# A decoder trunk on one core: three pool column tiles by groups of 256 tokens, early weights, a norm row by DMA, and three kept pairs of f tiles

## The chip, the core and the metric

The kernel runs on one core of a Trainium2 chip. The metric is the device time of one launch in microseconds; a time of the kernel is the median of several runs. The engines in the profile are PE (the matmul engine), DVE (vector), ACT (scalar), POOL (GpSimd) and SP, which here only issues DMAs.

## What is computed

One layer of a decoder on 1024 tokens of width 1024, in fp32. The input projection feeds three mixers; this is the reference cut to what the change touches:

```python
u = rmsnorm(x, norm_mix)
(pool_v, q, k, v, f_logit, z, xbc, dt_raw, gate_logits) = split_columns(u @ w_in)
y_pool = pool_mixer(pool_v, pool_mix, pool_scale) @ p_pool   # four groups of 128 columns
y_attn = forgetting_attention(q, k, v, f_logit, f_bias) @ p_attn
y_ssd  = ssd_mixer(z, xbc, dt_raw, ...) @ p_ssd
x = x + (g[0] * y_pool + g[1] * y_attn + g[2] * y_ssd) @ w_out
x = x + conv_ffn(rmsnorm(x, norm_ffn), ffn_up, ffn_conv_w, ffn_conv_b, ffn_down)
out = rmsnorm(x, norm_final)
```

The pool mixer takes, for each of its four groups, a trailing mean over 2, 4, 8 or 16 tokens, subtracts the token itself, multiplies by a 128 x 128 matrix and scales.

## The kernel before, in words

Every fp32 product is made of three matmuls on PE (`mm3`, L117): the high half of a weight with the high half of the data, the high half with the low, the low half with the high. A weight tile of 128 x 1024 comes by `load_w` (L107): SP issues its DMA into `wraw`, ACT casts it to `whi` (L112), DVE subtracts to `wlo` (L105). There is one `wraw` buffer, and there are three pairs of `whi` and `wlo`.

PSUM has two kinds of tiles here, set by `psum`: `big`, 1024 columns of fp32, which is two banks, and `bank`, 512 columns. Two of `big` and four of `bank` are set at first. A tile is taken when a buffer of its kind is free, and comes free with its last reader.

**The start (L207 to L228).** SP requests the eight tiles of x, 128 tokens each. The norm of a tile is a sum of squares on ACT (L150), a reciprocal root with a Newton step (`rstd`, L127 to L143, one column, mostly on DVE) and a product on DVE with the norm row (`n_xn`, L152). The norm row lies in `nm`, a `big` tile that four matmuls (L218) fill from a row of one partition. `to_T` turns the tile on PE, eight transposes into two `bank` tiles (L160); ACT casts the high half `uh` (L162) and DVE makes the low half `ul` (L105).

**Column tiles.** `in_proj` computes 128 columns of the projection for all tokens into one `big` tile, in groups of 512 tokens or of 256 (the first two pool tiles). After the second tile stand the f and dt projection (L303 to L393: softplus on DVE, then sums over tokens on PE, L362 to L366, copied by DVE into `acs`, `cum` and `tot`, and a running offset `off` that goes into `cum`).

**The pool mixers (L397 to L438).** For each of four groups: ACT copies the column tile out of PSUM to `va` (two buffers, L409), POOL makes the first shifted sum `vs` and DVE the others (L416), DVE makes the difference in `va` (L420). For each half of the tokens ACT casts `dh`, DVE makes `dl`, PE multiplies by the group's matrix into a `bank` tile (three matmuls: `dh` with `mixh`, `dl` with `mixh`, `dh` with `mixl`), ACT makes `yph` (L433) and DVE `ypl` (L435) from it. Then come the convolution tiles of the SSD mixer (`p_big`, in_proj again).

**The end (L1123 to L1237).** The FFN's down projection goes over eleven groups of f tiles, each a pair. For the last 512 tokens the last `NL` pairs are kept and `last_down` goes over them in two parts of 256 tokens, `qs[0]` and `qs[1]`, block by block (j = 4 to 7), each block with an add to x (L1224) and a square that goes into the sum of squares (L171, L172). `last_norm` makes the final norm of such a part: sums over partitions on PE (L179), the reciprocal root on DVE, its spread on PE (L185), eight products (L1187) and the output DMAs. `step` puts pieces of the norm of `qs[0]` among the blocks of `qs[1]`.

The order of the instructions on each engine is chosen by the framework's scheduler when the program is built; it is fixed in the program, and each engine goes through its own list.

## Time and profile before

| | us |
|---|---|
| median of three runs (lowest, highest) | 1877.31 (1876.27, 1879.17) |
| the profiled execution | 1876.14 |
| its span | 1874.4 |
| PE busy | 1841.7 (98%) |
| DVE busy | 1086.6 (58%) |
| ACT busy | 856.8 (46%) |

A row of the timeline gives the start in the span, the duration, and in brackets how long the engine stood idle before it and which instruction ended that. PE's matmuls overlap, so the distance between two starts, not the duration, is what one more costs. PEclk is the clock that PE was granted, 1.00 being full speed.

### The profile page before, as it was taken

The numbers are of one execution on the slowest core, as the hardware profiler recorded it, in microseconds if no ns is written. First come the engines' busy times: TensorE is split into PE (matmuls) and PEld (weight loads), VectorE is DVE, ScalarE is ACT, GpSimd is POOL, SyncE is SP. The second block draws the span as 40 slices with busy tenths as digits, with TensorE's granted clock in tenths as the row PEclk, the third lists the DMA queues.
The fourth block names the chain that finished last, engine by engine and source line by source line (L and its number), as shares of the span: only waits on it lengthen the run. The fifth ranks groups of instructions, "written<-read, shape, count | busy, mean of one in ns | idle before, by whom it ended". The sixth has DMA issues, their size and how long they took to land.

```text
span 1874.4 us, 22365 instructions
## 1 busy us (share of the span) xinstructions
PE 1841.7 (98%) x8622; PEld 1504.7 (80%) x8622; DVE 1086.6 (58%) x1611; ACT 856.8 (46%) x1384; POOL 157.1 (8%) x119
## 2 busy tenths in 40 slices
PE   7999999999999999999999999999999999999997
PEld 6888888888878778787788888878888888888886
DVE  6752682661265553655765432878787887743424
ACT  5343584573255463654633322545454555533221
POOL 0100240330000000000022002320000000000000
PEclk9999999999999999999999999999999999999998
DMA  4231231333511313124364451443333321664532
GB/s 153 84 120 34 85 108 57 101 130 104 175 65 62 107 51 129 40 90 153 121 200 135 145 180 68 152 135 124 102 107 118 104 91 53 214 235 157 180 102 68
DMA packets 81629, 217.35 MB, mean 116 GB/s; under 512 B 8625, under 2 KB 15217, under 8 KB 80754
## 3 DMA queue, kind: packets, MB, share of 16 engines
q1 hardware_dynamic: 76192, 201.82, 31.9%
q0 software_dynamic: 1728, 8.39, 1.4%
q10 hardware_dynamic: 3602, 5.72, 0.9%
q8 instruction: 67, 1.10, 0.2%
q14 instruction: 40, 0.33, 0.1%
HBM read 164.41 MB, written 51.48 MB: 115 GB/s over the span
## 4 chain that ended last, share of the span: by engine, by line
PE 93%; DVE 2%; DMA 2%; ACT 1%; issue 1%; POOL 0%; SPq 0%; DVEq 0%; ACTq 0%; POOLq 0%
PE p_bank L123 40%; PE p_big L123 19%; PE p_half L123 17%; PE p_bank L265 2%; PE p_bank L264 2%; PE p_bank L263 2%; PE p_po L722 2%; PE p_sc L674 2%; PE p_pt L697 2%; PE p_bank L557 1%; PE p_sc L673 1%; PE p_bank L1068 0%; DMA yi<-yn_d 0%; PE p_bank L324 0%; DMA ab<-in_f_up_dram 0%
## 5 line engine op out<-in xcount | busy, mean ns | idle before, releaser
L105 DVE TENSOR_TENSOR wlo<-wraw,whi 128x1024 fp32r<-128x1024 f32 (+1 forms) x109 | 126.3, 1159 | 162.8 <-ACT whi L112 161.3
L123 PE MATMUL p_bank<-act,whi 128*128 128x512 f32 (+1 forms) x736 | 218.5, 381 | 0.0
L123 PE MATMUL p_big<-uh,whi 128*128 128x512 f32 (+1 forms) x416 | 157.4, 379 | 0.5 <-ACT whi L112 0.5
L123 PE MATMUL p_big<-uh,wlo 128*128 128x512 f32 (+1 forms) x416 | 157.2, 378 | 0.5 <-DVE wlo L105 0.5
L123 PEld LDWEIGHTS p_bank<-act,whi 128*128 128x128 f32 x736 | 136.0, 188 | 26.6
L123 PE MATMUL p_big<-ul,whi 128*128 128x512 f32 (+1 forms) x416 | 156.7, 377 | 0.0
L123 PE MATMUL p_half<-uh,whi 128*128 128x512 f32 x384 | 153.4, 399 | 0.0
L123 PE MATMUL p_half<-ul,whi 128*128 128x512 f32 x384 | 153.0, 399 | 0.0
L123 PE MATMUL p_half<-uh,wlo 128*128 128x512 f32 x384 | 152.2, 397 | 0.0
L112 ACT CAST whi<-wraw 128x1024 fp32r<-128x1024 f32 x81 | 84.9, 1048 | 137.6 <-PE p_big L123 68.4
L123 PE MATMUL p_bank<-act,wlo 128*128 128x512 f32 (+1 forms) x368 | 139.2, 381 | 0.0
L123 PE MATMUL p_bank<-t,whi 128*128 128x512 f32 x440 | 137.2, 391 | 0.0
L123 PE MATMUL p_bank<-b,whi 128*128 128x512 f32 x376 | 118.9, 397 | 2.2 <-ACT whi L1046 2.0
L1024 DVE SCALAR_TENSOR_TENSOR vg<-cc,vec,vg 128x1023 f32<-128x1023 f32 (+1 forms) x88 | 110.3, 1278 | 8.4 <-ACT vg L1022 8.3
L105 DVE TENSOR_TENSOR wlo<-stage,whi 128x1024 fp32r<-128x1024 f32 x44 | 54.1, 1230 | 101.2 <-ACT whi L112 101.0
L112 ACT CAST whi<-stage 128x1024 fp32r<-128x1024 f32 x44 | 46.1, 1051 | 115.2 <-PE p_bank L123 106.7
L123 PEld LDWEIGHTS p_bank<-t,whi 128*128 128x128 f32 x440 | 82.6, 188 | 17.8
L123 PE MATMUL p_bank<-t,ring 128*128 128x512 f32 x396 | 96.4, 391 | 0.0
L172 POOL TENSOR_TENSOR ss<-ss,vg 128x512 f32<-128x512 f32 (+1 forms) x21 | 30.0, 1429 | 763.7 <-ACT vg L171 763.5
L123 PEld LDWEIGHTS p_big<-uh,wlo 128*128 128x128 f32 x416 | 78.9, 190 | 14.6 <-DVE wlo L105 0.8
L123 PEld LDWEIGHTS p_big<-uh,whi 128*128 128x128 f32 x416 | 79.0, 190 | 14.2 <-ACT whi L112 0.9
L123 PEld LDWEIGHTS p_big<-ul,whi 128*128 128x128 f32 x416 | 79.0, 190 | 13.5
(307 smaller groups left out, 4067.7 us busy)
## 6 DMA issues: line engine op xcount, KB each, us to landing
ab<-in_f_up_dram SPq DMA_DIRECT2D x53, 512.0 KB, 3.3
wraw<-in_w_in_dram SPq DMA_DIRECT2D x48, 512.0 KB, 3.4
stage<-in_f_down_dram SPq DMA_DIRECT2D x44, 512.0 KB, 3.5
g_d<-gt SPq DMA_DIRECT2D x48, 256.0 KB, 2.0
gt<-g_d SPq DMA_DIRECT2D x48, 256.0 KB, 3.4
act_d<-vg SPq DMA_DIRECT2D x22, 512.0 KB, 3.0
stage<-act_d SPq DMA_DIRECT2D x22, 512.0 KB, 4.5
mt<-acs_d SPq DMA_DIRECT2D x16, 512.0 KB, 4.4
```

The source lines that it names most:

```text
L105: eng.tensor_tensor(lo, src, hi.bitcast(F32), op=ALU.subtract)
L112: nc.scalar.copy(hi, raw)
L123: m = nc.tensor.matmul(o, lhsT=wt, rhs=ah[part], start=first and i == 0, stop=last and i == 2, **kw)
L172: eng.tensor_tensor(ss, ss, sq, op=ALU.add)
L263: nc.tensor.matmul(ps, lhsT=a, rhs=hi[:, c], start=k == 0, stop=False)
L264: nc.tensor.matmul(ps, lhsT=a, rhs=lo[:, c], start=False, stop=False)
L265: nc.tensor.matmul(ps, lhsT=ul[t // 4][:, k, q], rhs=hi[:, c], start=False, stop=k == NT - 1)
L557: nc.tensor.matmul(py[:, d], lhsT=mt[:, h * P:(h + 1) * P], rhs=xd[:, d], start=True, stop=True)
L674: nc.tensor.matmul(pss[:, 0:w], lhsT=Q2[h][hp, qs], rhs=KL[hp, j0:j0 + w], start=False, stop=True)
L697: nc.tensor.transpose(pt[:, off + (i - qq[0]) * P:off + (i - qq[0] + 1) * P], in_=probs[i][:, kb * P:(kb + 1) * P], identity=ident)
L722: nc.tensor.matmul(po[:, q0:q0 + w], lhsT=VV[:, kb, h, :], rhs=t[:, o:o + w], start=pc == 0 and i == 0, stop=last and i == len(prods) - 1)
L1024: nc.vector.scalar_tensor_tensor(out=acc[:, s:], in0=c[:, 0:1024 - s], scalar=w[2 - s], in1=acc[:, s:], op0=ALU.mult, op1=ALU.add)
```

## The change

Four things change. In the first stage PSUM is split into three `big` and two `bank` tiles; the old split comes back after the pool mixers. The norm row is spread to all partitions by a DMA into SBUF, and the four matmuls go. The weights of the first three pool tiles are requested behind the second, third and fourth tile of x, and these three tiles are computed together, group of 256 tokens by group; the third was computed by groups of 512 before. `in_proj` loses its width. At the end three pairs are kept instead of two, and the pieces of the norm of `qs[0]` stand after block 4, after block 5 and after blocks 6 and 7.

```diff
-    psum(big=(1024, 2), bank=(512, 4))
+    psum(big=(1024, 3), bank=(512, 2))
...
-    nm_row = spool.tile([1, 1024], F32, name="nm_row", bufs=1)
-    nc.scalar.dma_start(nm_row, row_in[:, R_NM:R_NM + 1024])
+    nm = spool.tile([P, 1024], F32, name="nm", bufs=1)
+    nc.scalar.dma_start(nm, row(R_NM, 1024))
...
-        nm = big()
-        for h in range(2):
-            nc.tensor.matmul(nm[:, h * 512:(h + 1) * 512], lhsT=ones[0:1, :], rhs=nm_row[:, h * 512:(h + 1) * 512],
-                             start=True, stop=True)
         xns = []
+        first_w = []
         for i in range(NT + 1):
             if i < NT:
                 xt = sp.tile([P, 1024], F32, name="xt", bufs=8)
                 nc.sync.dma_start(xt, x_t[i])
+                if i in (1, 2, 3):
+                    first_w.append(load_w(w_in[T_POOL + i - 1]))
                 xns.append(norm(sp, xt, nm, 4))
...
+        first = [big() for _ in first_w]
+        for t0 in range(0, S, 256):
+            h, q = t0 // 512, slice(t0 % 512, t0 % 512 + 256)
+            for ps, (hi, lo) in zip(first, first_w):
+                for k in range(NT):
+                    c = slice(k * P, (k + 1) * P)
+                    mm3([ps[:, t0:t0 + 256]], (hi[:, c], lo[:, c]), [(uh[h][:, k, q], ul[h][:, k, q])],
+                        k == 0, k == NT - 1)
         for g, w in enumerate(WINDOWS):
-            ps = in_proj(T_POOL + g, 256 if g < 2 else 512)
+            ps = first[g] if g < len(first) else in_proj(T_POOL + g)
...
+    psum(big=(1024, 2), bank=(512, 4))
...
-        NL = 2
+        NL = 3
...
-        m = step(m, last_down(qs[1], (5, 6)))
+        m = step(m, last_down(qs[1], (5,)))
         m = step(m, n)
-        m = step(m, last_down(qs[1], (7,)))
+        m = step(m, last_down(qs[1], (6, 7)))
```

SP's list now begins with two tiles of x, a weight, the other six tiles of x, the mixers' matrices and three weights; before, all eight tiles of x stood first. PE's list begins with 16 transposes ahead of the first column tile, where there were the four matmuls of L218 and 32 transposes.

Where the scheduler puts things further on is seen in three places. In the rows that follow, lines are those of each program; a number behind a name is that of its buffer's tile.

**PE in the pool mixers.** Here `p_big_909` and `p_big_954` are the fourth column tile, `p_big_1014` and `p_big_1067` the first convolution tile, and `p_bank_845`, `859`, `883` (before `783`, `797`) results of the mixers' products. Before:

```order
L123 MATMUL p_big_909<-uh1_85,wlo_906 128x512
L123 MATMUL p_big_1014<-uh0_84,whi_1010 128x512
L388 MATMUL p_bank_509<-cst_75,cumh_507 64x128
L123 MATMUL p_bank_783<-dh_779,mixh_524 128x512
L123 MATMUL p_big_1014<-ul0_86,whi_1010 128x512
L123 MATMUL p_big_1014<-uh0_84,wlo_1011 128x512
L123 MATMUL p_big_1014<-uh0_84,whi_1010 128x512
L123 MATMUL p_big_1014<-ul0_86,whi_1010 128x512
L123 MATMUL p_bank_783<-dl_781,mixh_524 128x512
L123 MATMUL p_bank_783<-dh_779,mixl_526 128x512
L123 MATMUL p_bank_797<-dh_793,mixh_524 128x512
L123 MATMUL p_big_1014<-uh0_84,wlo_1011 128x512
```

After:

```order
L123 MATMUL p_big_954<-uh1_85,wlo_951 128x512
L385 MATMUL p_bank_524<-cst_75,acs_360 128x128
L123 MATMUL p_bank_845<-dh_841,mixh_539 128x512
L123 MATMUL p_bank_845<-dl_843,mixh_539 128x512
L123 MATMUL p_bank_845<-dh_841,mixl_541 128x512
L123 MATMUL p_bank_859<-dh_855,mixh_539 128x512
L123 MATMUL p_bank_859<-dl_857,mixh_539 128x512
L123 MATMUL p_bank_859<-dh_855,mixl_541 128x512
L123 MATMUL p_bank_883<-dh_879,mixh_539 128x512
L123 MATMUL p_bank_883<-dl_881,mixh_539 128x512
L123 MATMUL p_bank_883<-dh_879,mixl_541 128x512
L123 MATMUL p_big_1067<-uh0_84,whi_1063 128x512
```

Before, the products of the second group stand among the matmuls of the convolution tile. After, the products of three halves follow each other, between the fourth column tile and the convolution tile.

**DVE in the pool mixers**, from the copy of the sums on (`acs`, `cum`, `tot`). Before:

```order
L370 COPY acs_345<-p_bank_483 128x128
L371 COPY cum_349<-p_bank_483 128x64
L368 COPY tot_487<-p_bank_485 128x192
L375 TENSOR_TENSOR off_491<-off_491,tot_487 128x8
L380 TENSOR_TENSOR dd_503<-tot_487,acs_345 128x128
L375 TENSOR_TENSOR off_491<-off_491,tot_487 128x8 x3
L382 TENSOR_TENSOR dtd_347<-dtt_344,dd_503 128x128
L375 TENSOR_TENSOR off_491<-off_491,tot_487 128x8
L416 TENSOR_TENSOR vs_868<-vs_865 128x1024
L375 TENSOR_TENSOR off_491<-off_491,tot_487 128x8
L416 TENSOR_TENSOR vs_871<-vs_868 128x1024
```

After:

```order
L368 COPY acs_360<-p_bank_498 128x128
L369 COPY cum_364<-p_bank_498 128x64
L366 COPY tot_502<-p_bank_500 128x192
L423 TENSOR_TENSOR vs_916<-vs_913 128x1024
L421 MEMSET vs_1006 128x16
L373 TENSOR_TENSOR off_506<-off_506,tot_502 128x8
L378 TENSOR_TENSOR dd_518<-tot_502,acs_360 128x128
L105 TENSOR_TENSOR wlo_1188<-wraw_1185,whi_1187 128x1024
L425 TENSOR_TENSOR vs_916<-vs_916,cst_75 128x16
L421 MEMSET vs_1009 128x16
L373 TENSOR_TENSOR off_506<-off_506,tot_502 128x8
L442 SCALAR_TENSOR_TENSOR ypl_851<-p_bank_845,vec_82,yph_849 128x512
```

After the copies now come a weight's low half and a second shifted sum before the first `ypl`; six rows further, `va_907`, and then `ypl_865` and `dl_895`, follow.

**DVE at the end**, where the norm of `qs[0]` and the last blocks meet. Before:

```order
L1224 TENSOR_TENSOR x2h_13376<-x2h_13376,p_bank 128x256
L140 TENSOR_TENSOR rs_t<-rs_t,rs_v 128x2
L141 TENSOR_SCALAR rs_t<-rs_t 128x2
L143 TENSOR_TENSOR rs_r<-rs_y,rs_t 128x2
L172 TENSOR_TENSOR ss<-ss,vg 128x256
L1224 TENSOR_TENSOR x2h_13376<-x2h_13376,p_bank 128x256
L1187 SCALAR_TENSOR_TENSOR x2h_13376<-x2h_13376,vec,p_st 128x256 x8
L172 TENSOR_TENSOR ss<-ss,vg 128x256
L1224 TENSOR_TENSOR x2h_13376<-x2h_13376,p_bank 128x256
L172 TENSOR_TENSOR ss<-ss,vg 128x256
```

After:

```order
L141 TENSOR_SCALAR rs_t<-rs_t 128x2
L1232 TENSOR_TENSOR x2h_13429<-x2h_13429,p_bank 128x256
L143 TENSOR_TENSOR rs_r<-rs_y,rs_t 128x2
L172 TENSOR_TENSOR ss<-ss,vg 128x256
L1195 SCALAR_TENSOR_TENSOR x2h_13429<-x2h_13429,vec,p_st 128x256 x8
L1232 TENSOR_TENSOR x2h_13429<-x2h_13429,p_bank 128x256 x2
L172 TENSOR_TENSOR ss<-ss,vg 128x256 x2
L181 TENSOR_REDUCE rs_n<-p_st 128x2
```

L1187 has become L1195 and L1224 has become L1232. The add of a block now stands right ahead of L143, the last step of the reciprocal root, and two adds stand behind the eight products, with their sums of squares after them.

## Rows read from the trace of the kernel before

**Rows 1.** The page: busy time of each engine; the last chain, by engine.

```profile
PE 1841.7 (98%) x8622; PEld 1504.7 (80%) x8622; DVE 1086.6 (58%) x1611; ACT 856.8 (46%) x1384; POOL 157.1 (8%) x119
...
PE 93%; DVE 2%; DMA 2%; ACT 1%; issue 1%; POOL 0%; SPq 0%; DVEq 0%; ACTq 0%; POOLq 0%
```

**Rows 2.** Waits of PE in 0 to 130 us: total, times, longest, us.

```profile
PE p_big L218 <- DMA cst<-in_cst_dram: 6.8, 1, 6.8
PE p_bank L160 <- DVE n_xn L152: 2.8, 2, 1.4
PE p_bank L160 <- DVE rs_y L134: 2.3, 1, 2.3
```

**Rows 3.** Windows: length; busy of PE, PEld, DVE, ACT, POOL; PEclk; DMA; GB/s.

```profile
20.00:25.00 5.00, 4.06 (x18) 3.36 (x17) 4.85 (x12) 3.38 (x8) 0.00 (x0) 0.50 0.27 88
...
35.00:40.00 5.00, 3.73 (x32) 3.77 (x33) 4.33 (x9) 2.42 (x4) 0.00 (x0) 1.00 0.40 128
```

**Rows 4.** PE instructions by group, 0 to 36.2 us; xcount, busy, mean ns.

```profile
L160 PE MATMUL p_bank<-cst,n_xn 128*128 128x128 f32 x56 | 9.7, 330 | 3.7 <-DVE rs_y L134 2.3 <-DVE n_xn L152 1.4
L123 PE MATMUL p_big<-uh,whi 128*128 128x256 f32 x24 | 7.6, 319 | 0.5 <-ACT whi L112 0.5
```

**Rows 5.** Timeline: start, us, instruction, [idle before]; PE's last early wait.

```profile
36.27 1.06 PE L160 MATMUL p_bank<-cst,n_xn 128*128 128x128 f32 x8 [1.44 <-DVE n_xn L152]
```

**Rows 6.** Timeline of PE: neighbouring matmuls of 256 and of 512 columns.

```profile
27.54 0.28 PE L123 MATMUL p_big<-uh,whi 128*128 128x256 f32 x1
27.66 0.28 PE L123 MATMUL p_big<-ul,whi 128*128 128x256 f32 x1
...
63.00 0.39 PE L123 MATMUL p_big<-ul,whi 128*128 128x512 f32 x1
...
63.23 0.39 PE L123 MATMUL p_big<-uh,wlo 128*128 128x512 f32 x1
```

**Rows 7.** Timeline of DVE in the start.

```profile
25.50 1.28 DVE L152 SCALAR_TENSOR_TENSOR n_xn<-xt,rs_r,p_big 128x1024 f32<-128x1024 f32 x1
...
26.99 1.23 DVE L105 TENSOR_TENSOR wlo<-wraw,whi 128x1024 fp32r<-128x1024 f32 x1
...
29.39 0.69 DVE L105 TENSOR_TENSOR ul<-p_bank,uh 128x512 fp32r<-128x512 f32 x1
```

**Rows 8.** The page, DMA issues: KB each, us to landing.

```profile
mt<-acs_d SPq DMA_DIRECT2D x16, 512.0 KB, 4.4
```

**Rows 9.** Timeline in the pool mixers: DVE, then PE, then ACT.

```profile
56.33 1.51 DVE L345 TENSOR_SCALAR den<-e 128x192 f32<-128x192 f32 x1 [0.33 <-ACT e L343]
...
74.86 0.29 DVE L370 COPY acs<-p_bank 128x128 f32<-128x128 f32 x1 [0.29 <-PE p_bank L364]
...
78.48 1.23 DVE L416 TENSOR_TENSOR vs<-vs 128x1024 f32<-128x1024 f32 x1
...
79.98 1.22 DVE L420 SCALAR_TENSOR_TENSOR va<-vs,va 128x1024 f32<-128x1024 f32 x1
...
81.25 0.74 DVE L435 SCALAR_TENSOR_TENSOR ypl<-p_bank,vec,yph 128x512 fp32r<-128x512 f32 x1
...
85.41 0.39 PE L123 MATMUL p_big<-uh,whi 128*128 128x512 f32 x1
...
86.33 1.01 ACT L409 COPY va<-p_big 128x1024 f32<-128x1024 f32 x1
```

**Rows 10.** Busy us by engine around a PE wait in the FFN; PEclk.

```profile
886.00:887.00 1.00, 0.23 (x1) 0.00 (x0) 0.37 (x2) 0.98 (x3) 0.00 (x0) 1.00 1.00 303
...
889.00:890.00 1.00, 1.00 (x5) 0.70 (x5) 0.00 (x0) 0.00 (x0) 0.00 (x0) 0.50 1.09 410
```

**Rows 11.** Timeline of the last tokens: DVE and PE.

```profile
1859.78 3.22 DVE L1187 SCALAR_TENSOR_TENSOR x2h<-x2h,vec,p_st 128x256 f32<-128x256 f32 x8
...
1860.78 0.28 PE L123 MATMUL p_bank<-act,wlo 128*128 128x256 f32 x1
...
1863.25 0.41 DVE L1224 TENSOR_TENSOR x2h<-x2h,p_bank 128x256 f32<-128x256 f32 x1
```

More of the change, by code (lines that the diff above doesn't have):

```diff
@@ L228, in hybrid_kernel, with in_proj @@
                 to_T(xns[t], uh[t // 4], ul[t // 4], (t % 4) * P)
-    def in_proj(t, width=512, after=None):
+    def in_proj(t, after=None):
         hi, lo = load_w(w_in[t], after=after)
         ps = big()
-        for t0 in range(0, S, width):
-            h, q = t0 // 512, slice(t0 % 512, t0 % 512 + width)
+        for h in range(2):
             for k in range(NT):
                 c = slice(k * P, (k + 1) * P)
-                mm3([ps[:, t0:t0 + width]], (hi[:, c], lo[:, c]), [(uh[h][:, k, q], ul[h][:, k, q])],
+                mm3([ps[:, h * 512:(h + 1) * 512]], (hi[:, c], lo[:, c]), [(uh[h][:, k, :], ul[h][:, k, :])],
                     k == 0, k == NT - 1)
```

## The prediction

> **What bounds the kernel now.** I read the page's busy shares and its chain of waits first [rows 1]: the matmul engine, PE, is busy for 1841.7 of 1874.4 us, and 93% of the chain that ends last lies on it. So an edit counts where it fills a hole of PE, opens one, or gives PE more to do. The list of PE's waits in the first 130 us gives the holes there [rows 2]: 6.8 us until the constants land, 2.8 and 2.3 us for the norm of x, and two of 0.5 us that are left out of the rows. All of them lie before 37 us; in the pool mixers PE runs without a hole today. The window table gives the state of PE's clock at the start [rows 3]: 0.50 of full speed, the lower of its two levels (1.2 of 2.4 GHz), in 20 to 25 us, right behind the 2.3 us hole, and full again later, as in 35 to 40 us.
>
> **The start: more work early, a little more work in all.** Before, PE leaves its last hole at 36.27 us [rows 5], with 24 matmuls of each of three kinds, 72 of 256 columns, and 56 transposes done [rows 4]. In the changed program the first matmul of a column tile stands behind 16 transposes instead of 32, and its weight is the third transfer on SP's queue. That start should come at some 14 to 15 us, but there is only one raw weight buffer, and the low half of the second weight is row 46 of DVE's queue. Ahead of it DVE has six norm products at 1.28 us, two low halves of weights at 1.23, six of x at 0.69 [rows 7], one of the mixers' matrix at about the same, and some 27 one-column operations at about 0.15: 7.7 + 2.5 + 4.1 + 0.7 + 4.0 = 19.0 us. The first product can start at about 6.8 us, so this half is there at 25 to 26 us; by the program's order PE then has only 27 matmuls and 32 transposes behind it. From there both tiles' groups keep PE fed. The missing 45 matmuls cost 45 x 0.12 = 5.4 us (27.54 to 27.66 in [rows 6]) and the missing 24 transposes 24 x 0.12 = 2.9 (eight in 1.06 less the tail of the last one, [rows 5]). PE is level with the old 36.27 at about 33.6 to 34: a gain of 2.3 to 2.7 us. Against it stands the narrower third tile: 48 matmuls of 512 columns become 96 of 256, and by [rows 6] a pair takes 0.24 against 0.23, so 48 x 0.01 = 0.5 us. The clock is the open term: short holes remain between 20 and 25 us, and at half speed until 28 instead of 25 PE would lose up to 1.6. The gain lies between 0.2 and 2.2 us; I take 1.2.
>
> The norm row now comes to all partitions by one DMA of 512 KB on ACT's queue, in place of four matmuls. The nearest row is a 512 KB read that is spread over the partitions in the same way, 4.4 us from issue to landing [rows 8]. Issued at 0.7 us it would land at 5 if alone; beside the x tiles, at up to 8, and the constants behind it follow. DVE then begins up to 1.2 us later and the whole start with it. So this term reaches from -2.2 to +1.0 us.
>
> **The pool mixers: a new hole.** This is the largest term. Three column tiles now hold three wide PSUM buffers, and only two banks are left for transposes, the f and dt work, and the mixers' products, where there were four. One of the two is held by the small tile with the summed decays (L385, then L388) until its last copy on DVE. The mixers' four first products therefore follow each other in the other bank. PE's queue has L385, then nine product matmuls in a row, and then the first convolution tile; before, its six products stood among the matmuls of the fourth tile.
>
> When does PE get there? Before, the convolution tile's first matmul starts at 85.41 [rows 9], with six product matmuls (1.4 us) and L387 ahead of it. Without these, and with 2.5 us gained at the start, PE ends the fourth tile at about 81.2 us. When does DVE? Before, it copies the sums at 74.86 and is free at once. After, the softplus chain starts later, because the f and dt matmuls stand behind three column tiles instead of two, by about 6.4 us; a mixer product va (1.22) and a shifted sum vs (1.23) of the next tiles stand ahead of the copy as well; a wait of DVE that was there before (2 us) is filled. So the copies come at about 82.3 us. Rows in which DVE takes 1.51 us for 192 columns while GpSimd adds [rows 9] lie in that stretch too, and three such additions crowd in.
>
> From the copies to the low half dl that frees the buffer va, DVE must do in this order: acs 0.29, cum 0.21, tot 0.35, vs 1.23, four short ones 0.6, dd 0.28, a weight's low half 1.23, ypl 0.74, dl 0.67, dtd 0.28, va 1.22, ypl 0.74, dl 0.67, in sum 8.5 us, and some 0.4 less since they overlap a little (those over a microsecond and ypl are in [rows 9], the weight's half in [rows 7], the short ones are read from the same view). It ends at about 90.4. Then ACT copies the fourth tile into va, 1.01 us [rows 9], and only that frees the wide buffer in which the convolution tile is to start: 91.4 us. Between 81.2 and 91.4 PE has L385 (0.1) and nine product matmuls (9 x 0.23 = 2.1, [rows 6]) to do. The hole is 10.2 - 2.2 = 8.0 us. It comes in four parts: about 1.6 us for the copy of cum, 3.0 for the first ypl, 2.1 for the second, 1.2 for the copy into va. Queued behind PE's waiting instruction is the whole convolution, which needs none of these results; nothing later gives the time back, as PE had no holes there that could shrink. If DVE comes to the copies earlier or later by 1 us, the hole is 7 to 9.
>
> The clock may add to this. After an idle stretch of 1.4 us at 886 us, in the middle of dense work, the granted clock was 0.50 until 892, some three microseconds, though PE was busy throughout [rows 10]; it was 0.50 after the 2.3 us hole at the start too [rows 3]; after the 1.44 us hole before 36.27 it stayed full [rows 3, 5]. Half speed for 3.4 us of dense work costs 1.7, and if two of the products run slow as well, 1.2 more, since DVE waits for them. Bounds 0 to 2.9; I take 1.7, the row at 886.
>
> The Trainium skill ("TensorE: Matmul & The Clock Gate", "A second HAM failure mode: psum-queue depth-cycling") says that cycling through PSUM banks makes PE idle briefly between groups of matmuls, often enough that the clock swings between its levels and throughput falls. The change halves the banks in this stretch, so the rule speaks against it. By it the sum would take the upper end of the clock's term instead of the middle.
>
> **The tail.** Three pairs of f tiles instead of two are kept for the last 512 tokens. That turns 24 matmuls of 512 columns into 48 of 256: 24 x 0.01 = 0.25 us more. The two steps of the second half that follow the first half's norm now hold 36 matmuls instead of 12, so that the eight products of the norm (3.22 us, from 1859.78) lie beside PE work. Before, the last matmul starts at 1860.78 and ends at 1861.06, but its add stands behind these eight and a sum of squares and starts at 1863.25 [rows 11]. After, the add follows at once: -2.1 us. Against that, the last step of the reciprocal root (L143) now stands behind the add of block 5, and PE's L185 waits for it: an add 0.41 (as in [rows 11]), a small product 0.16, and two hand-overs make 0.7 us. Net -2.1 + 0.25 + 0.7 = -1.15; between -0.5, if the last weight's halves come late, and -1.6, if PE's last short matmuls keep the full clock. I take -1.2. The third kept weight needs the buffer of the last group before it; other matmuls cover its cast and its low half, 1.0 and 1.2 us, with 28 or more ahead of them in PE's queue (3.3 us); without that cover it would cost up to 2.3.
>
> **The sum.** Start -1.2, hole +8.0, clock +1.7, tail -1.2: +7.3 us. The profiled execution took 1876.14 us, so 1883.4 by it; it is 1.2 below the median of the runs, 1877.31, so 1884.6 on that. I say 1884.5. All good ends together (-2.2, +7.0, 0, -1.6) give 1880.5, all bad ones (+1.0, +9.0, +2.9, -0.5) 1889.7.
>
> **Rivals.**
> *The hole is covered (faster side).* If DVE reached the copy of cum by some 73 to 74 us, as it does now, the ypl and dl would be done before PE ends the fourth tile, and only start and tail would remain: 1877.3 - 1.2 - 1.2 = 1874.9, at best 1877.3 - 2.2 - 1.6 = 1873.5. For it: before, DVE was busy for only 7.6 of 10 us in the 70s. Against it: the f and dt matmuls come 6.4 us later, and PE's order leaves nothing between L385 and the convolution. DVE would have to be 8 us earlier than its own list allows. Chance 0.10.
> *Half the hole.* DVE is ahead by three or four microseconds, since operations overlap more than I count or GpSimd blocks it less: 1877.3 - 2.4 + 4 = about 1879, not to be told from no change. Chance 0.12.
> *The hole without the clock.* PE stays at full clock: 1884.6 - 1.7 = 1882.9. It lies in the forecast's own range. This and the forecast together have 0.71.
> *The start loses.* The spread row lands at 8 us or later, the first norms queue behind it, and the half clock lasts until 28: +1.0 or more instead of -1.2, and with the upper end of the clock in the mixers 1888 to 1891. Chance 0.07.
> *The change doesn't bring the early start that it describes*, because the one raw buffer and DVE's order hold the second weight until 25 us: this is in the sum already, as the small gain.
>
> About 0.2%, or 3.75 us, is what a measurement of this kernel can tell from no change: slower begins above 1881.1, faster below 1873.6. Of the covered hole (0.10) half may fall below that. So faster 0.05, same 0.19 (the other half of it, half the hole, and a little of the forecast's lower end), slower 0.76. The range, 1878.5 to 1889, leaves out the covered hole and the worst of the start.
>
> **What would show it.** In the profile after: PE's list of waits between 80 and 92 us with some 8 us, for DVE's cum and ypl and ACT's va (right), or nothing there (wrong); the convolution tile's first matmul near 91 to 93 us instead of 85.41; a granted clock of 0.50 in a window near 85 to 96 us; the second weight's low half at 25 to 26 us and the last hole of the start before 31; in the tail an add right behind PE's last matmul, and a PE wait of about 0.7 us for L143. The prediction is wrong if DVE's copies come by 75 us, or if PE has anything to do between the products.

## The result, and the profile after

The changed kernel takes 1889.71 us, the median of four runs (1889.6 to 1891.38), against 1877.82 for the kernel before: 11.9 us more, a ratio of 1.0066 (95% interval 1.0048 to 1.0083). I had said 1884.5, from 1878.5 to 1889.0. It is slower, as forecast, and mainly by the mechanism that I named, but by 5.2 us more than I said, 0.7 above the range. (The 1877.82 is the median of four runs, the three of the first table and one more.) The profiled execution took 1891.38 us, its span 1889.6.

The page's busy shares hide this. PE is busy for 5.7 us more than before [rows 1], since the change brings narrower matmuls and stretches at half clock; the rest is waiting. After the page's row, the list of PE's waits in 0 to 130 us (total, times, longest) shows where:

```profile
PE 1847.4 (98%) x8690; PEld 1512.1 (80%) x8690; DVE 1087.4 (58%) x1611; ACT 858.3 (45%) x1384; POOL 156.6 (8%) x119
```

```profile
PE p_bank L160 <- DVE rs_v L130: 10.3, 2, 9.7
PE p_bank L385 <- DVE cum L369: 3.3, 1, 3.3
PE p_bank L160 <- DVE ul L105: 2.7, 2, 2.2
PE p_bank L123 <- DVE ypl L442: 2.4, 1, 2.4
PE p_big L123 <- DVE wlo L105: 1.6, 1, 1.6
PE p_bank L123 <- DVE vs L421: 1.6, 1, 1.6
...
```

The waits for `cum`, `ypl` and `vs` are new against [rows 2]: they lie in the pool mixers, where PE had no hole. The first matmul of the projection behind the mixers gives the sum of all that happens ahead of it. Its row of before, then of after:

```profile
144.33 0.39 PE L263 MATMUL p_bank<-whi,uh 128*128 128x512 f32 x1
```

```profile
157.08 0.39 PE L261 MATMUL p_bank<-whi,uh 128*128 128x512 f32 x1
```

That is 12.75 us later, and the loss lies ahead of 101 us, where the clock is full again. The changed tail gives 1.6 back, which makes 11.1, for 11.9 in the medians. The two profiled executions themselves lie 15.2 us apart (spans of 1889.6 and 1874.4), since the one of after is the slowest of its four and the one of before the fastest. These other 4.1 us come up between the projection and the tail, where PE's granted clock was below full three times in the profile of after (0.72 in 900 to 905 us, 0.77 in 920 to 925, 0.66 in 1240 to 1245) and once in that of before (at 889 [rows 10]). `e_tail` below, which has the order of before there, shows such a fall in 1225 to 1230 too, so I do not put them down to the change.

**The pool mixers.** The timeline of PE between the fourth column tile, whose last matmul starts at 84.85, and the convolution tile (start, us, instruction, idle before it):

```profile
84.85 0.39 PE L123 MATMUL p_big<-uh,wlo 128*128 128x512 f32 x1
88.54 0.30 PE L385 MATMUL p_bank<-cst,acs 128*128 128x128 f32 x1 [3.30 <-DVE cum L369]
...
92.11 0.79 PE L123 MATMUL p_bank<-dh,mixh 128*128 128x512 f32 x1 [2.36 <-DVE ypl L442]
...
95.32 0.80 PE L123 MATMUL p_bank<-dh,mixh 128*128 128x512 f32 x1 [1.56 <-DVE vs L421]
...
97.10 0.80 PE L123 MATMUL p_big<-uh,whi 128*128 128x512 f32 x1
```

The products go through one bank, each a good 3.2 us behind the one before, as DVE and ACT empty it. (The wait that is put down to a small row of `vs` ends with the second `ypl`, at 95.26.) From 85.1 to 97.1 PE has 2.2 us of work at full clock, so the hole is 9.8 us. The windows of the same stretch (columns as in [rows 3]) give the clock: half of full speed from 90 to 100.

```profile
90.00:95.00 5.00, 1.65 (x3) 0.83 (x3) 4.55 (x11) 2.38 (x5) 0.00 (x0) 0.50 0.66 198
95.00:100.00 5.00, 4.54 (x10) 3.15 (x11) 4.12 (x13) 2.16 (x3) 1.89 (x1) 0.50 0.59 218
```

What the hole waits for is DVE's copy of the sums. The rows of ACT, POOL and DVE ahead of it show a chain that I had not seen:

```profile
82.75 1.05 ACT L112 CAST whi<-wraw 128x1024 fp32r<-128x1024 f32 x1 [4.82 <-DMA wraw<-in_w_in_dram]
83.70 1.01 ACT L416 COPY va<-p_big 128x1024 f32<-128x1024 f32 x1
...
84.78 2.02 POOL L423 TENSOR_TENSOR vs<-va 128x1024 f32<-128x1024 f32 x1 [10.96 <-ACT va L416]
...
86.84 1.22 DVE L423 TENSOR_TENSOR vs<-vs 128x1024 f32<-128x1024 f32 x1 [1.78 <-POOL vs L423]
87.98 0.28 DVE L368 COPY acs<-p_bank 128x128 f32<-128x128 f32 x1
```

ACT's copy of the third tile stands behind the cast of a later weight, which waits 4.82 us for its DMA into the one raw buffer. POOL waits for the copy, DVE for POOL, and the copy of `acs` stands behind that shifted sum: the copy comes at 87.98 instead of 74.86 [rows 9]. PE had ended the sums by 84.1, itself 9 us later than before; the last 3.9 us are DVE's list.

**The start.** Rows of DVE (the first norm product, the second weight's low half) and PE, then the windows:

```profile
8.39 1.28 DVE L152 SCALAR_TENSOR_TENSOR n_xn<-xt,rs_r,nm 128x1024 f32<-128x1024 f32 x1
...
25.12 1.22 DVE L105 TENSOR_TENSOR wlo<-wraw,whi 128x1024 fp32r<-128x1024 f32 x1
...
26.40 0.58 PE L123 MATMUL p_big<-uh,wlo 128*128 128x256 f32 x1 [1.61 <-DVE wlo L105]
```

```profile
25.00:30.00 5.00, 3.60 (x17) 3.60 (x18) 4.90 (x15) 1.94 (x5) 0.00 (x0) 0.50 0.31 108
30.00:35.00 5.00, 5.00 (x37) 5.00 (x37) 3.55 (x4) 1.73 (x3) 0.00 (x0) 0.82 0.31 101
```

The first tile of x is used 1.8 us later than before (5.95 for 4.15), beside the spread row; even so the first norm product comes at 8.39 instead of 10.63, since it no longer waits for the constants and PE. The second weight's low half ends at 26.3, PE's last early wait with it. But then PE runs at half speed to about 31.8 us: half of 3.60 and 0.18 of 5.00 make 2.7 us. PE ends the fourth tile at 85.1; before, it would have at 83.9 (85.41 [rows 9], less 1.5 for the products and L387 that stood ahead). So the start loses 1.2 us.

**The tail.** PE's waits from 1840 us on, of before, then from 1860 us of after, and three rows of after's DVE and PE:

```profile
PE p_st L179 <- DVE ss L172: 3.7, 1, 3.7
PE p_st L185 <- DVE rs_r L143: 2.0, 1, 2.0
```

```profile
PE p_st L185 <- DVE rs_r L143: 2.6, 2, 2.0
PE p_st L179 <- DVE ss L172: 1.5, 1, 1.5
```

```profile
1873.29 0.42 DVE L1232 TENSOR_TENSOR x2h<-x2h,p_bank 128x256 f32<-128x256 f32 x1 [0.17 <-PE p_bank L123]
1873.63 0.15 DVE L143 TENSOR_TENSOR rs_r<-rs_y,rs_t 128x2 f32<-128x2 f32 x1
...
1873.84 0.43 PE L185 MATMUL p_st<-cst,rs_r 128*128 128x128 f32 x2 [0.58 <-DVE rs_r L143]
```

The wait behind the eight products is 2.2 us shorter; the new one, for L143 behind an add, is 0.58.

### The profile page after: what moved, and what is told of

It is laid out like the page before. It is cut to its first block, busy times and chain, and to the rows that moved or that the text cites. A ratio compares the mean times of both kernels' runs of the same rounds, so it can differ in the third digit from the quotient of the medians.

```text
span 1889.6 us, 22501 instructions
## 1 busy us (share of the span) xinstructions
PE 1847.4 (98%) x8690; PEld 1512.1 (80%) x8690; DVE 1087.4 (58%) x1611; ACT 858.3 (45%) x1384; POOL 156.6 (8%) x119
## 3 DMA queue, kind: packets, MB, share of 16 engines
q0 software_dynamic: 1728, 8.39, 1.4%
## 4 chain that ended last, share of the span: by engine, by line
PE 91%; DVE 3%; DMA 2%; ACT 2%; issue 1%; POOL 0%; SPq 0%; DVEq 0%; ACTq 0%; POOLq 0%
PE p_bank L123 40%; PE p_big L123 18%; PE p_half L123 16%; PE p_bank L263 2%; PE p_bank L262 2%; PE p_bank L261 2%; PE p_po L730 2%; PE p_sc L682 2%; PE p_pt L705 2%; PE p_sc L681 1%; PE p_bank L565 1%; DMA wraw<-in_w_in_dram 1%; DVE wlo L105 1%; DMA yi<-yn_d 0%; PE p_bank L1076 0%
## 5 line engine op out<-in xcount | busy, mean ns | idle before, releaser
L123 PE MATMUL p_big<-uh,wlo 128*128 128x512 f32 (+1 forms) x432 | 161.4, 374 | 1.6 <-DVE wlo L105 1.6
L123 PE MATMUL p_big<-uh,whi 128*128 128x512 f32 (+1 forms) x432 | 161.8, 375 | 0.9 <-ACT whi L112 0.8
L123 PE MATMUL p_big<-ul,whi 128*128 128x512 f32 (+1 forms) x432 | 160.9, 373 | 0.1
L123 PEld LDWEIGHTS p_big<-uh,whi 128*128 128x128 f32 x432 | 83.2, 193 | 15.4 <-ACT whi L112 1.0
L123 PEld LDWEIGHTS p_big<-uh,wlo 128*128 128x128 f32 x432 | 83.1, 192 | 15.1 <-DVE wlo L105 1.8
L123 PEld LDWEIGHTS p_big<-ul,whi 128*128 128x128 f32 x432 | 83.2, 193 | 13.3 <-DVE rs_t L141 0.4
```

The costliest lines, as they stand in the source:

```text
L123: m = nc.tensor.matmul(o, lhsT=wt, rhs=ah[part], start=first and i == 0, stop=last and i == 2, **kw)
```

## The experiments

### The tail alone, and all but the tail

`e_tail` is the kernel before with the change's last two hunks (`NL = 3`, the pieces of the norm after blocks 4, 5 and 6 with 7); `e_notail` is the changed kernel without them.

> The kernel before with the change at the end alone: three kept pairs of f tiles and the blocks in the order 4, 5, 6 and 7. My theory (the end gains what its late add was waiting for): the add of the last block follows PE's last matmul at once, -1.2 to -1.6 us, so about 1876.4 where before is 1877.8. Rival (the end brings nothing, and the whole difference lies at the start): 1877.8. Either way PE's waits in the first 130 us are those of before.

> The changed kernel with the end of the kernel before: start and pool mixers alone. My theory (all of the loss lies before 105 us, some 1 us in the start and some 11 in the mixers): 1877.8 + 12.7 = 1890.5, a little above the changed kernel. Rival (the loss lies in what follows, in the attention and the FFN, where the two traces also drift apart by 4 us): the first convolution tile is late by the same 12 us, but the total differs from this by several microseconds.

`e_tail` takes 1874.9 us, a ratio of 0.999 (0.9981 to 0.9998); `e_notail` 1890.48, 1.0071 (1.0058 to 1.0084). So the tail is a small gain by itself (0.4 to 3.6 us by its interval, where I had expected 1.2 to 1.6), about what its waits say, and the whole loss is in the rest, as I had expected of `e_notail`.

### The old PSUM split later

In `e_late` the old split, two wide buffers and four banks, comes back later than in the changed kernel, only behind the second convolution tile, so that the products stand among convolution matmuls; all else is the changed kernel.

```diff
-    psum(big=(1024, 2), bank=(512, 4))
...
+            if g == 0:
+                psum(big=(1024, 2), bank=(512, 4))
```

> The changed kernel, but the split of PSUM into two wide tiles and four banks comes back after the second convolution tile instead of ahead of the first. The first convolution tile can then take a wide buffer that has long been read, and 45 of its matmuls stand around the first product in PE's queue; there are still only two banks for the products. My theory (the hole is there because the convolution tile has to wait for the fourth tile's buffer, so that nothing but products can stand in PE's queue): the hole of 9.8 us and the half clock behind it (1.4) go, at most 2 us stay; 1878 to 1880. Rival 1 (two banks are too few wherever the split comes back): the products hold up PE as before, 1888 or more. Rival 2 (the loss lies in the start): 1889.

1883.42 us, 1.0032 (1.002 to 1.0044): 6.3 us better than the changed kernel, but 3 to 5 short of what I expected. The copy of `acs` is just as late (87.82), and L385 starts at 89.00 without a wait, because PE has the convolution tile to do meanwhile. But other waits stand 25 us later (PE, 80 to 130 us):

```profile
PE p_big L123 <- DVE acc L463: 2.6, 1, 2.6
PE p_bank L123 <- DVE ypl L442: 1.2, 1, 1.2
```

So with DVE just as late, another order of PE's list takes away half of the loss; the other half stays.

### Two early tiles and no third wide buffer

`e_two` requests only two weights early and keeps the old PSUM split throughout.

```diff
-    psum(big=(1024, 3), bank=(512, 2))
+    psum(big=(1024, 2), bank=(512, 4))
...
-                if i in (1, 2, 3):
+                if i in (1, 2):
```

> The changed kernel with two early column tiles instead of three, two wide PSUM tiles and four banks throughout; the third and the fourth tile are computed by groups of 512 as before. My theory: no hole in the mixers; the start as in the changed kernel, within 1 us of before, since DVE's list still holds up the second weight's low half until about 26 us; the end gains 1.6; in sum 1876 to 1878. Rival (the early weights and the spread row cost the time by themselves): 1885 or more.

1881.58 us, 1.0023 (1.0014 to 1.0032); I had expected 1876 to 1878. With four banks there is no wait from 30 to 109 us, and then one of 6 us, for the wide buffer of the third convolution tile, with half clock behind it (0.50 from 115 to 120 us). PE's wait, and ACT's row that starts the work on the first convolution tile's result:

```profile
115.70 0.77 PE L123 MATMUL p_big<-uh,whi 128*128 128x512 f32 x1 [6.06 <-DVE acc L463]
...
110.41 1.20 ACT L459 ACTIVATE acc<-p_big,vec 128x1024 f32<-128x1024 f32 x1
```

ACT comes to `acc` 5.2 us late (105.19 before), behind the results of late products and the cast of a weight. Here it is not the number of banks. DVE's copy of the sums comes at 78.41, 3.6 us later than before, where the changed kernel has it 13.1 later; PE meets this smaller lateness at another place. Since this run changes the number of early tiles and the split together, it does not tell the two apart.

### All eight products ahead of the convolution

`e_swap` sets the old split back in the other order, so that the convolution's buffer comes last and all eight products stand ahead of it, in one row.

```diff
-    psum(big=(1024, 2), bank=(512, 4))
+    psum(bank=(512, 4), big=(1024, 2))
```

> The changed kernel with the two kinds of tiles named in the other order where the old PSUM split comes back, so that the first convolution tile lands on the banks of the mixers' products. All eight products then stand ahead of the convolution in PE's queue, instead of three. My theory (each product ahead of the convolution tile costs PE a round trip over ACT and DVE, 3.2 us from one ypl to the next in the changed kernel's trace, less the 0.7 of its own work): five more of them, 5 x 2.5 = 12.5 us, and a little more for the half clock and for the sums of the third and fourth tile: 1902 to 1906. Rival (the hole is a single late event, and what stands behind it is free): 1890.

1900.86 us in its one run, a little below the 1902 to 1906 that I expected: 11 us more than the changed kernel for five more products in the row. By the projection (165.43 for 157.08) it is 8.4 us, about 1.7 for each, with PE's clock at 0.50 from 90 to 110 us; where the rest belongs, one run does not tell. PE's waits from 80 to 130 us:

```profile
PE p_bank L385 <- DVE cum L369: 3.5, 1, 3.5
PE p_bank L123 <- ACT dh L433: 3.4, 1, 3.4
PE p_bank L123 <- DVE ypl L442: 2.3, 2, 1.8
...
```

The first wait is as it was (3.3 in the changed kernel), and the products that were added wait for DVE and ACT in their turn. So here a row of products with nothing between them costs PE what these two engines need for each.

### One buffer more

`e_va3` gives `va` three buffers, so that ACT's copy of the fourth tile, and with it the convolution, need not wait for the products; `e_two2_va3` does the same for two early tiles and puts the casts of the convolution tiles' weights behind the `acc` of two tiles before.

```diff
-            va = pp.tile([P, 1040], F32, name="va")
+            va = pp.tile([P, 1040], F32, name="va", bufs=3)
```

> The changed kernel with three buffers instead of two for va, the mixers' copy of a column tile. The copy of the fourth tile then waits for no low half dl, and the convolution tile stands ahead of the products in PE's queue; the split of PSUM comes back at the same place, with two banks for the products. My theory (it was the full va that kept the fourth tile in PSUM, and so kept the convolution tile out): no wait of PE between 80 and 105 us. But the scheduler now puts the last five products in a row between the second and the third convolution tile, and there a new hole comes, five round trips of some 2.3 us each less what is hidden, 6 to 9 us: 1884 to 1888. Rival 1 (the two banks are the cause): a hole at the same place as in the changed kernel, 1889. Rival 2 (five products in a row do no harm when DVE is no longer late): 1879.

> Two early column tiles as in the run with two, but with three buffers for va, and the casts of the third and later convolution weights on ACT issued behind the first steps (acc) of the convolution tile two before, so that these no longer stand behind a cast that waits. In the run with two early tiles PE had one wait of 6.1 us for a wide PSUM tile that DVE had not finished reading, and half clock for 6.5 us behind it, 9.3 us in sum, while all else was 2.7 us ahead of before. My theory: this wait shrinks to 0 to 3 us, without the half clock: 1877.5 - 2.5 (end) - 2.7 (start) + 0 to 3 = 1872 to 1875. Rival (the wait only moves to another place, as DVE's whole list is late): 1879 or more.

`e_va3`: 1890.61 us, 1.0075 (1.0061 to 1.0089), no gain. The first hole is nearly gone, and another stands before the third convolution tile, where I expected it, but larger, with the clock at 0.50 in 120 to 125 us behind it (waits of PE, 80 to 130 us):

```profile
PE p_big L123 <- DVE acc L465: 5.9, 1, 5.9
...
```

`e_two2_va3`: 1878.89 us, 1.0012 (1.0003 to 1.002). Its wait for `acc` is 4.4 us, my expectation of 1872 to 1875 fell, and the rival's 1879 came. (The casts that I moved put a low half of a weight, 1.21 us, among the adds of `acc`, so this run does not show the third buffer alone.) In both the wait moves when one limit is taken away; for `e_va3` that was part of my theory, whose 1884 to 1888 was 2.6 us too low. So no single one of these buffers was the cause, and my theory up to here, that the two banks make the hole, was too narrow.

### The softplus sooner

In the changed kernel the early tiles finish together and the f and dt matmuls stand behind most of their groups. They start 9 us later than before, and the softplus 10 us, on a DVE that stood idle (rows of before, then of after). With two early tiles (`e_two`) the softplus is only 1.7 us late, at 55.01.

```profile
42.07 0.28 PE L324 MATMUL p_bank<-uh,wfh 128*56 128x256 f32 x1
...
53.35 0.36 DVE L336 TENSOR_TENSOR y<-p_bank,bias 128x192 f32<-128x192 f32 x1 [13.97 <-PE p_bank L329]
```

```profile
51.08 0.28 PE L322 MATMUL p_bank<-uh,wfh 128*56 128x256 f32 x1
...
63.29 0.36 DVE L334 TENSOR_TENSOR y<-p_bank,bias 128x192 f32<-128x192 f32 x1 [14.76 <-PE p_bank L327]
```

`e_fdt` and `e_two_fdt` change only that: the later groups of the early tiles, from the second tile of the third group on, are issued behind the last f and dt matmul, `fd`. The first has three early tiles and the changed kernel's PSUM, the second two early tiles, as `e_two`.

```diff
-            nc.tensor.matmul(pt[:, t * 24:(t + 1) * 24], lhsT=fdT[0:56, t * P:(t + 1) * P], rhs=fold,
+            fd = nc.tensor.matmul(pt[:, t * 24:(t + 1) * 24], lhsT=fdT[0:56, t * P:(t + 1) * P], rhs=fold,
...
-            for ps, (hi, lo) in zip(first, first_w):
+            for j, (ps, (hi, lo)) in enumerate(zip(first, first_w)):
+                with tc.issue_after(fd.ins) if t0 + j > 512 else nullcontext():
```

> The changed kernel, with the f and dt projection ahead of the last five of the twelve groups of the early tiles, so that the softplus no longer waits for all three tiles; PSUM and the products stay as in the changed kernel, with nine and more product matmuls still in a row. Theory (the hole is DVE's debt: softplus began at 63.3 us instead of 53.4, while DVE had stood idle for 14.8 us before it): softplus begins at 53 to 56 us, the copy of acs comes before 82 us instead of 87.98, the waits of PE between 80 and 100 us fall from 10 us to at most 3 and with them the stretch at half clock behind them; 1880 to 1883 us. Rival 1 (the one bank through which the products go sets the hole, at 2.2 us per product, whenever DVE starts): 8 us or more of waits stay between 85 and 105 us; 1888 to 1892. Rival 2 (the wait only moves on to the third convolution tile, as in the kernels before): 4 to 6 us there with some half clock; 1884 to 1887.

> Two early tiles with the old PSUM split, which took 1881.6 us, with the f and dt projection ahead of the last three of their eight groups. Theory (late softplus is the cause): the 6.1 us wait for the third convolution tile's buffer and the 3.2 us of half clock behind it go for the most part; 1873 to 1876 us. Rival (acc of the first convolution tile is late for another reason, the products that bunch up): 4 us or more remain; 1878 to 1882.

`e_fdt`: 1885.05 us, 1.0038 (1.0023 to 1.0052). The softplus and the copy of `acs` (DVE), and PE's waits between 85 and 93 us:

```profile
57.84 0.36 DVE L334 TENSOR_TENSOR y<-p_bank,bias 128x192 f32<-128x192 f32 x1 [10.59 <-PE p_bank L327]
...
73.57 0.28 DVE L368 COPY acs<-p_bank 128x128 f32<-128x128 f32 x1
...
85.99 0.30 PE L386 MATMUL p_bank<-cst,cumh 128*64 128x128 f32 x1 [0.50 <-DVE cumh L383]
87.82 0.62 PE L123 MATMUL p_bank<-dh,mixh 128*128 128x512 f32 x1 [1.54 <-DVE rows L389]
90.75 0.77 PE L123 MATMUL p_bank<-dh,mixh 128*128 128x512 f32 x1 [1.46 <-DVE ypl L443]
```

With the softplus 5.5 us sooner the copy comes 14.4 us sooner, since it no longer stands behind the shifted sum that waited for POOL. PE's waits there go from 7.2 us to 3.5, and the hole, counted as before, from 9.8 to 5.7. What is left, though the copy now comes sooner than the 74.86 of before, is the row of products through one bank, with half clock behind it (0.52 from 90 to 95 us). The time lies above the theory's 1880 to 1883 and inside the second rival's 1884 to 1887, but that rival's place, the third convolution tile, has no wait. So the theory is right for about half of the hole: the copies came early, as it said, but the half clock and 3.5 us of waits stayed, and the one bank, which the first rival held for the whole cause, makes the rest.

`e_two_fdt`: 1877.1 us, 1.0 (0.999 to 1.0009), against 1881.58 for `e_two`; I had expected 1873 to 1876. There is no wait of PE between 27 and 140 us, and the projection starts at 141.12 instead of 144.33. The softplus starts at 49.57, not only in time but 3.8 us sooner than before the change. The start of the projection in `e_fdt`, then in `e_two`, then in `e_two_fdt`, beside the 157.08 of the changed kernel:

```profile
150.80 0.39 PE L261 MATMUL p_bank<-whi,uh 128*128 128x512 f32 x1
```

```profile
150.92 0.39 PE L261 MATMUL p_bank<-whi,uh 128*128 128x512 f32 x1
```

```profile
141.12 0.39 PE L261 MATMUL p_bank<-whi,uh 128*128 128x512 f32 x1
```

At the projection, the sooner softplus alone gives 6.3 us back, two early tiles with the old split alone 6.2, and both together 16.0. But `e_two_fdt` does not end 3.2 us sooner than the kernel before: it loses between 941 and 1003 us, where the order of PE had come out differently (waits in 930 to 1010 us; before, there was one of 0.2 us there):

```profile
PE p_bank L818 <- DVE yi L814: 2.3, 3, 1.3
PE p_big L123 <- DVE mg L628: 1.8, 1, 1.8
```

`e_two_fdt_va3` is the same kernel with a third `va` buffer. PE's order in the mixers stays, and the order behind the attention becomes that of `e_nmtail`, below.

> Two early tiles with the f and dt projection ahead of the last three of their eight groups, as in the kernel before it, and a third va buffer; this leaves the order of PE in the mixers as it was and brings the order behind the attention back to that of the kernel with the spread norm row and the tail alone. Theory (the 3.2 us that the kernel without the third buffer had gained by 144 us were lost behind the attention, between 941 and 1003 us, where its order differs, and not in the mixers): the gain of 3 us at 144 us stays to the end and the tail adds 1.6 to 1.9; 1871 to 1874 us. Rival (the gain at the start is always given back later, since the clock dips and the waits of the attention grow with it): 1876 to 1878.

1872.3 us, 0.9977 (0.9967 to 0.9987), as expected, which is faster than both kernels and the lowest median here, though its interval overlaps that of `e_nmtail`. The projection starts at 140.42, 3.9 us ahead of before, and the span (1867.9) ends 6.5 ahead, 1.6 of it by the tail; this execution was the fastest of its nine. PE has no wait from 30 to 140 us. DVE's copy:

```profile
67.16 0.27 DVE L368 COPY acs<-p_bank 128x128 f32<-128x128 f32 x1
```

### Without early weights, and with one

`e_nmtail` is the kernel before with the spread norm row and the tail; `e_one2` adds one early weight, with the casts as in `e_two2_va3`.

> The kernel before with the new end and the norm row spread by DMA, and no early weights, no third early tile, the old PSUM split. My theory (the spread row starts DVE's first product 2 us sooner, 8.4 instead of 10.6 us, although x lands later, and DVE's list is what bounds the start): 1.5 to 2 us better than the new end alone, which is 1874.9: 1873. Rival (the row's 512 KB delay x by 2 us and this eats the gain): 1875.

> Only the first pool tile's weight is requested early, with the old PSUM split, the spread norm row and the three kept pairs; the casts of the convolution tiles' weights stand behind the acc two tiles before. Theory (tiles that finish together are the cause, and one early tile does not finish later than before): no wait over 2 us in the mixers, the start some 0 to 2 us better than with the spread row alone; 1872 to 1875 us. Rival (every early weight costs the start, since its low half and the cast stand ahead of the norms): 1876 to 1878.

`e_nmtail`: 1874.47 us, 0.9985 (0.9976 to 0.9994), with the projection 2.4 us sooner than before and no wait in the mixers. But that is only 0.4 us below the 1874.9 of `e_tail`, less than the runs can tell apart, and nearer the rival's 1875 than my 1873: the whole time shows no gain of the spread row. `e_one2`: 1879.27, 1.001 (1.0 to 1.0019), above both of its expectations. Its softplus is on time (53.91, for 53.35 before), its start gained (PE has some 30 more matmuls of 256 columns done when the f and dt matmuls start), and yet PE waits 3.5 us for `acc` at the third convolution tile. A row of DVE there, between the first and the second add of `acc`, then PE's:

```profile
107.73 1.22 DVE L105 TENSOR_TENSOR wlo<-wraw,whi 128x1024 fp32r<-128x1024 f32 x1
...
111.60 0.47 PE L124 MATMUL p_big<-uh,whi 128*128 128x512 f32 x1 [3.53 <-DVE acc L466]
```

The casts that I had moved put a weight's low half among the adds of `acc`; that is some 1.2 of the 3.5 us. The rest is that ACT starts `acc` at 105.30, as before (105.19), behind the last products, while PE is ready for the third tile at 108.1. What this kernel would take without the moved casts was not run.

## Why the prediction was wrong in size

*The mixers' hole*, forecast 8.0: 9.8. The mechanism held, with the products in a row, the waits for `cum`, `ypl` and what frees `va`, and the convolution queued behind. Two steps of its timing failed. The f and dt chain was not 6.4 us late but 9.9: I counted the third tile's matmuls ahead of it, and missed that the last transposes of x also stand among the column groups, so that the f and dt matmuls start at 51.08 instead of 42.07, behind some 70 more matmuls of 256 columns (8.4 us at 0.12). And where I had a wait of DVE of 2 us filled, 1.4 of it stayed (for a cast, at 83.83), and a new one of 1.78 us came, at the end of the chain of DMA, cast, copy and POOL. Together the copies come at 88.0, not 82.3: 5.7 late. That the hole is only 1.8 longer comes from PE, which reached it 3.9 us later than I said (85.1 for 81.2).

The hole ends with DVE, so the failed step is the time of DVE's copies: the convolution starts at 97.10 and not at the 91.4 that I added up, late by the same 5.7 us, and what PE loses ahead of a hole makes it shorter. My sum hid some of this: it works out the hole with PE 2.5 us early and takes the start at 1.2, so 1.3 us of hole are counted too much. How far PE's later start adds to the lateness of the copies, through the f and dt matmuls, no run shows.

*What makes it.* I named the banks first, and they are about half of it. The sooner softplus alone took 4.7 us off the changed kernel's median; a PSUM split that changes behind the second convolution tile, and so another order of PE with DVE as late as ever, 6.3; two early tiles with the old split 8.1; these and the sooner softplus 12.6, and 17.4 with one more buffer. So two things make the loss: a late DVE, and a row of products through one bank that makes PE pay for it at once. Either one alone still costs: with DVE early (`e_fdt`) the row leaves a hole of 5.7 us, and with two early tiles and four banks a softplus 1.7 us late goes with 6 us of waiting. Three early tiles with the sooner softplus and the later split were not run together.

*The clock behind the hole*, forecast 1.7: 1.5. The first seven matmuls of the convolution took 3.08 us instead of the 1.6 of seven at 0.23, which is 1.5 us more. The three products before them ran slow as well, inside the waits. The Trainium skill ("TensorE: Matmul & The Clock Gate", "A second HAM failure mode: psum-queue depth-cycling") says that cycling through PSUM banks can make PE idle between groups of matmuls so often that its clock swings between its two levels. The trace agrees so far that the clock was 0.50 from 90 to 100 us while the products went through one bank; it shows one such stretch and no swinging, and its price was near the middle of my range and not its upper end of 2.9.

*The start*, forecast a gain of 1.2 with a range from 2.2 gained to 1.0 lost: 1.2 us lost. The step that failed is the clock's, of which the value held 0.8 and the bound 1.6: it took 2.7. The low half of the second weight ended at 26.3, 0.3 behind my 25 to 26; PE had done the 27 matmuls and 32 transposes that I counted by then. That it came so near is in part luck: DVE's first product started at 8.39 and not at 6.8, which is more than the 1.2 us of delay that I allowed for the spread row, and the list from there took 18.0 us and not 19.0. From the mean of what I said, 33.8 us for being level with the old 36.27, 0.8 for the weight and 2.7 for the clock make 37.3, and the narrower tile's 0.5 brings the loss to some 1.5, near the 1.2 seen. Against the kernel before, the spread row makes the first product 2.2 us sooner, and the projection 2.4 us sooner in `e_nmtail`; a gain in the whole time is not shown.

*The tail*, forecast 1.2 of gain: 1.6 in the trace; the medians of the two pairs differ by 2.6 (`e_tail`) and 0.8 (`e_notail`, less than those runs can tell apart). Each step is there, 2.2 for 2.1 and 0.58 for 0.7.

The measured sum is +1.2 + 9.8 + 1.5 - 1.6 = 10.9, for 11.9 in the medians; the last 1.0 is put down to no place. The bad ends of my own terms made 1889.7, which is what came, but my range stopped short of them. The rivals on the faster side, *the hole is covered* and *half the hole*, needed DVE to be sooner than its list; it was 5.7 us later. *The start loses* came nearest, with its 1888 to 1891, in part by luck: the half clock at the start lasted to 31.8, past its 28, but its spread row landed at 6.1 us and not at 8, and what it wanted from the clock in the mixers came from a longer hole.

## What to carry to other kernels

Work that starts early can cost more than it gains where several tiles then finish together: ask which engine must take up their results, when its own chain can begin, and place the small matmuls that feed that chain ahead of the bulk. If taking away one buffer limit only moves a wait, look for the engine that is late, and for a second limit beside it. And a gain at the start counts only when the profile at the end still has it, since an order that a scheduler plans can change hundreds of microseconds further on.

## What the runs showed of the hardware

After waits of much the same length the clock did not do the same. Behind 1.61 us at 26.40 it was 0.50 in the changed kernel; behind 1.44 us at the same place in `e_va3`, where PE's start has another order, it stayed full (1.00 in 25 to 30 us). It differs even where PE's order is the same: the wait for a weight's cast at 1223 us, 2.01 us in the kernel before and 1.84 in `e_tail`, was followed by a lower clock in `e_tail` alone (window of before, then of `e_tail`):

```profile
1225.00:1230.00 5.00, 5.00 (x24) 4.13 (x23) 4.95 (x4) 2.32 (x4) 5.00 (x2) 1.00 0.82 247
```

```profile
1225.00:1230.00 5.00, 5.00 (x16) 3.93 (x16) 3.61 (x4) 1.62 (x3) 5.00 (x2) 0.66 0.73 251
```

So a hole is best priced twice, once with the clock and once without. A DMA of 512 KB that spreads one row took 5.4 us from issue to landing beside the tiles of x, against the 4.4 of the nearest row of before [rows 8].
